# Batch norm with ReLU: all stores issued from GpSimd's queue in place of ScalarE's

## Chip, cores and metric

One core of a Trainium2 chip. The time is the device time of one execution in microseconds (us), the median of several, at a granted clock of 1.00. A profile is one execution under the hardware profiler; its span is the time from the first to the last instruction.

## The reference

```python
def setup_inputs():
    batch, channels, h, w = 32, 128, 32, 32
    # x (32,128,32,32) normal; gamma 1, beta 0, mean 0, var 1 (each of 128 channels); eps 1e-5

def reference(x, gamma, beta, running_mean, running_var, eps):
    normalized = (x - running_mean[None, :, None, None]) / np.sqrt(running_var[None, :, None, None] + eps)
    scaled = normalized * gamma[None, :, None, None] + beta[None, :, None, None]
    return np.maximum(scaled, 0).astype(np.float32)
```

16.78 MB of float32 are read, one multiply-add and a maximum made of each element, and 16.78 MB written.

## The kernel before

An image and channel is one row of 1024 elements; a partition holds 16 rows, and t numbers the two halves of the tensor. The first half is loaded in tiles that grow from 1 to 4 MB, the second as one 8 MB tile in two loads. All loads are issued from SyncE, the last by 8.5 us. ScalarE computes each tile in place and then issues its store; only the first tile has two stores. One store or load is cut into descriptors, pieces of 4 to 64 KB, which 16 transfer engines work through.

```python
J = 16
TILES = ((0, 0, 2), (0, 2, 4), (0, 4, 8), (0, 8, 16), (1, 0, 16))
LOAD_CUTS = {(1, 8)}
STORE_CUTS = {(0, 1)}
HALVES = {(0, 0), (0, 1)}
# ...
    for t, a, b in TILES:
        xt = data.tile([P, b - a, HW], F32, name=f"x{t}_{a}")
        cuts = [a] + [j for j in range(a + 1, b) if (t, j) in LOAD_CUTS] + [b]
        for c, d in zip(cuts, cuts[1:]):
            nc.sync.dma_start(out=xt[:, c - a : d - a, :], in_=xr[t, :, c:d, :])
        tiles.append((t, a, b, xt))
# ... scale_t and bias_t, one column per row, from the four parameters: done by 9.6 us
    with tc.manual_schedule(engines={mybir.EngineType.Activation}):
        for t, a, b, xt in tiles:
            first = a
            for j in range(a, b):
                step = HW // 2 if (t, j) in HALVES else HW
                for w in range(0, HW, step):
                    nc.scalar.activation(
                        out=xt[:, j - a, w : w + step], in_=xt[:, j - a, w : w + step],
                        func=ACTF.Relu, bias=bias_t[:, j : j + 1], scale=scale_t[:, j : j + 1],
                    )
                if j + 1 == b or (t, j + 1) in STORE_CUTS:
                    nc.scalar.dma_start(
                        out=outr[t, :, first : j + 1, :], in_=xt[:, first - a : j + 1 - a, :]
                    )
                    first = j + 1
```

Of the kernel before, what the change touches and what calls it, by code (L numbers as in the profile page):

```python
# [1 line left out]

# [4 lines left out]


F32 = mybir.dt.float32
ACTF = mybir.ActivationFunctionType  # L10
# [13 lines that stand above are left out]
@with_exitstack  # L24
def kernel(
    ctx: ExitStack,
    tc: tile.TileContext,
    x: bass.AP,
    gamma: bass.AP,
    beta: bass.AP,  # L30
    running_mean: bass.AP,
    running_var: bass.AP,
    eps: bass.AP,
    out: bass.AP,
):
    nc = tc.nc
    B, C, H, W = x.shape
    HW = H * W
    P = nc.NUM_PARTITIONS
    assert C % J == 0 and P % (C // J) == 0 and (B * C) % (P * J) == 0  # L40
    Q = C // J
    T = B * C // (P * J)

    xr = x.rearrange("b c h w -> (b c) (h w)").rearrange("(t p j) w -> t p j w", p=P, j=J)
    outr = out.rearrange("b c h w -> (b c) (h w)").rearrange("(t p j) w -> t p j w", p=P, j=J)

    data = ctx.enter_context(tc.tile_pool(name="data", bufs=1))
    params = ctx.enter_context(tc.tile_pool(name="params", bufs=1))
    psum = ctx.enter_context(tc.tile_pool(name="psum", bufs=1, space=bass.MemoryType.PSUM))

    tiles = []
# [9 lines that stand above are left out]
    raw = params.tile([Q, 4, J], F32, name="raw")  # L61
    for k, src in enumerate((running_var, gamma, running_mean, beta)):
        nc.scalar.dma_start(out=raw[:, k, :], in_=src.rearrange("(q j) -> q j", j=J))
    eps_t = params.tile([P, 1], F32, name="eps_t")
    nc.vector.memset(eps_t, float(eps))  # L65
    rep = params.tile([Q, P // Q, Q], F32, name="rep")
    nc.gpsimd.memset(rep, 1.0)  # L67
    nc.gpsimd.affine_select(  # L68
        out=rep,
        in_=rep,  # L70
        compare_op=mybir.AluOpType.is_equal,
        fill=0.0,
        base=0,
        pattern=[[0, P // Q], [-1, Q]],
        channel_multiplier=1,
    )
    cols = psum.tile([P, 4, J], F32, name="cols")
    nc.tensor.matmul(  # L78
        cols.rearrange("p k j -> p (k j)"),
        rep.rearrange("q r s -> q (r s)"),  # L80
        raw.rearrange("q k j -> q (k j)"),
        start=True,
        stop=True,
    )
    std_t = params.tile([P, J], F32, name="std_t")
    nc.scalar.activation(out=std_t, in_=cols[:, 0, :], func=ACTF.Sqrt, bias=eps_t[:, 0:1], scale=1.0)  # L86
    rstd_t = params.tile([P, J], F32, name="rstd_t")
    nc.vector.reciprocal(out=rstd_t, in_=std_t)  # L88
    scale_t = params.tile([P, J], F32, name="scale_t")
    nc.vector.tensor_mul(out=scale_t, in0=cols[:, 1, :], in1=rstd_t)  # L90
    ms_t = params.tile([P, J], F32, name="ms_t")
    nc.vector.tensor_mul(out=ms_t, in0=cols[:, 2, :], in1=scale_t)  # L92
    bias_t = params.tile([P, J], F32, name="bias_t")
    nc.vector.tensor_sub(out=bias_t, in0=cols[:, 3, :], in1=ms_t)  # L94

    with tc.manual_schedule(engines={mybir.EngineType.Activation}):
        for t, a, b, xt in tiles:
            first = a
            for j in range(a, b):
# [3 lines that stand above are left out]
                        out=xt[:, j - a, w : w + step],  # L103
                        in_=xt[:, j - a, w : w + step],
                        func=ACTF.Relu,
                        bias=bias_t[:, j : j + 1],
                        scale=scale_t[:, j : j + 1],
                    )
                if j + 1 == b or (t, j + 1) in STORE_CUTS:
                    nc.scalar.dma_start(  # L110
                        out=outr[t, :, first : j + 1, :], in_=xt[:, first - a : j + 1 - a, :]
                    )
                    first = j + 1


# [1 line left out]
_INS = ['x', 'gamma', 'beta', 'running_mean', 'running_var', 'eps']  # L117
_OUTS = [((32, 128, 32, 32), 'float32')]

_NUMBERS = {'eps': 1e-05}  # L120


# [26 lines left out]
```

## Time and profile before

| | before |
|---|---|
| time, three runs ahead of the prediction | 83.94 us (83.65 to 83.94) |
| span of the profile | 82.0 us |
| first load data, last store data (transfer records) | 1.80 us, 80.80 us |
| ScalarE busy | 39.1 us |
| loads and stores, share of the 16 transfer engines | 48.7% and 47.6% |
| last load ends, last store is issued | 46.2 us, 56.05 us |

How to read it: transfers are named by queue (q1 is SyncE's, q10 ScalarE's), and a queue's share is the time that its descriptors took on the 16 engines. The most useful view was the one that takes the queues in a chosen stretch of time: it shows what waits behind what. Its counts go by the start of a descriptor, so a short stretch can show over 100%. Two words are used below: the **stream** is the time from the first load data to the last store data, 79.00 us here, and the **close** is what follows to the end of the span, 1.17 us here. Both are taken from the trace's transfer records. A store's **landing** is the moment at which its semaphore is up: for the last store 0.34 us after its last data, so inside the close.

### The profile page before, as it was taken

What the parts mean: (1) busy time and instruction counts of PE and PEld (TensorE: products, weight loads), DVE (VectorE), ACT (ScalarE), POOL (GpSimd) and SP (SyncE); (2) the same over time, 40 slices, a digit from 0 to 9 for tenths busy, and PEclk for the clock granted to TensorE, in tenths of its full rate; (3) what the DMA queues carried; (4) which work ended last, traced back from release to release, by engine and by line L of the source; (5) the groups of instructions that cost most, each with busy time, mean ns of one, the idle gap of its engine ahead of it and who ended that gap; (6) DMA issues with size and microseconds to landing.
All of it is one profiled execution on the core that took longest, in us unless ns stands there. A gap on an engine that the chain in (4) does not pass through costs nothing.

```text
span 82.0 us, 120 instructions
## 1 busy us (share of the span) xinstructions
PE 0.7 (1%) x2; PEld 0.5 (1%) x2; DVE 0.8 (1%) x5; ACT 39.1 (48%) x36; POOL 0.8 (1%) x6
## 2 busy tenths in 40 slices
PE   0002000000000000000000000000000000000000
PEld 0002000000000000000000000000000000000000
DVE  0000300000000000000000000000000000000000
ACT  0600477799239999199994199993000000000000
POOL 3000000000000000000000000000000000000000
DMA  2899997979899989999799799998992999996590
GB/s 48 336 424 456 416 544 336 524 322 526 338 434 430 506 358 506 390 434 444 320 460 500 316 424 448 512 432 368 480 736 128 416 512 512 512 512 288 224 512 0
DMA packets 1792, 33.56 MB, mean 409 GB/s; under 512 B 256, under 2 KB 256, under 8 KB 512
## 3 DMA queue, kind: packets, MB, share of 16 engines
q1 hardware_dynamic: 864, 16.78, 48.7%
q10 hardware_dynamic: 928, 16.78, 47.6%
HBM read 16.78 MB, written 16.78 MB: 409 GB/s over the span
## 4 chain that ended last, share of the span: by engine, by line
DMA 56%; ACT 10%; issue 2%; SPq 0%
DMA x<-in_x_dram 56%; ACT x L102 10%; SPq L56 0%
## 5 line engine op out<-in xcount | busy, mean ns | idle before, releaser
L102 ACT ACTIVATE x<-x,bias_t,scale_t 128x1024 f32<-128x1024 f32 (+1 forms) x34 | 37.5, 1177 | 9.9 <-DMA x<-in_x_dram 7.6
L86 ACT ACT_TABLE_LOAD x1 | 1.3, 1283 | 2.6 <-issue 2.6
L86 ACT ACTIVATE std_t<-cols,eps_t 128x16 f32<-128x16 f32 x1 | 0.3, 273 | 4.5 <-PE cols L78 4.5
L78 PE MATMUL cols<-raw,rep 8*128 8x64 f32 x2 | 0.7, 429 | 7.6 <-DMA raw<-in_beta_dram 7.6
L78 PEld LDWEIGHTS cols<-raw,rep 8*128 8x128 f32 x2 | 0.5, 306 | 7.6 <-issue 7.6
L68 POOL TENSOR_SCALAR_AFFINE_SELECT rep<-rep 8x128 f32<-8x128 f32 x1 | 0.4, 392 | 0.1
L88 DVE RECIPROCAL rstd_t<-std_t 128x16 f32<-128x16 f32 x1 | 0.3, 254 | 7.7 <-ACT std_t L86 7.7
L67 POOL MEMSET rep<- 8x128 f32 x1 | 0.2, 194 | 0.3 <-POOLq L130 0.3
L90 DVE TENSOR_TENSOR scale_t<-cols,rstd_t 128x16 f32<-128x16 f32 x1 | 0.2, 175 | 0.1
L92 DVE TENSOR_TENSOR ms_t<-cols,scale_t 128x16 f32<-128x16 f32 x1 | 0.2, 175 | 0.0
L94 DVE TENSOR_TENSOR bias_t<-cols,ms_t 128x16 f32<-128x16 f32 x1 | 0.2, 174 | 0.0
L130 POOL MEMSET const-bfloat16-1.0<- 128x1 bf16 x1 | 0.1, 106 | 0.0
L130 POOL MEMSET const-uint8-127<- 128x1 uint8 x1 | 0.1, 106 | 0.0
L130 POOL MEMSET const-float32-0.0<- 128x1 f32 x1 | 0.1, 103 | 0.3 <-issue 0.3
L130 POOL MEMSET const-float32-1.0<- 128x1 f32 x1 | 0.1, 103 | 0.0
L65 DVE MEMSET eps_t<- 128x1 f32 x1 | 0.1, 59 | 0.9 <-PEq L130 0.9
## 6 DMA issues: line engine op xcount, KB each, us to landing
x<-in_x_dram SPq DMA_DIRECT2D x3, 4096.0 KB, 38.7
out_dram<-x ACTq DMA_DIRECT2D x1, 4096.0 KB, 28.7
x<-in_x_dram SPq DMA_DIRECT2D x2, 1024.0 KB, 5.8
x<-in_x_dram SPq DMA_DIRECT2D x1, 2048.0 KB, 11.3
out_dram<-x ACTq DMA_DIRECT2D x1, 2048.0 KB
out_dram<-x ACTq DMA_DIRECT2D x2, 512.0 KB, 19.6
out_dram<-x ACTq DMA_DIRECT2D x1, 1024.0 KB
raw<-in_running_var_dram ACTq DMA_DIRECT2D x1, 0.5 KB
```

Of the source, the lines that this page charges most:

```text
L65: nc.vector.memset(eps_t, float(eps))
L67: nc.gpsimd.memset(rep, 1.0)
L68: nc.gpsimd.affine_select(out=rep, in_=rep, compare_op=mybir.AluOpType.is_equal, fill=0.0, base=0, pattern=[[0, P // Q], [-1, Q]], channel ...
L78: nc.tensor.matmul(cols.rearrange("p k j -> p (k j)"), rep.rearrange("q r s -> q (r s)"), raw.rearrange("q k j -> q (k j)"), start=True, s ...
L86: nc.scalar.activation(out=std_t, in_=cols[:, 0, :], func=ACTF.Sqrt, bias=eps_t[:, 0:1], scale=1.0)
L88: nc.vector.reciprocal(out=rstd_t, in_=std_t)
L90: nc.vector.tensor_mul(out=scale_t, in0=cols[:, 1, :], in1=rstd_t)
L92: nc.vector.tensor_mul(out=ms_t, in0=cols[:, 2, :], in1=scale_t)
L94: nc.vector.tensor_sub(out=bias_t, in0=cols[:, 3, :], in1=ms_t)
L102: nc.scalar.activation(out=xt[:, j - a, w : w + step], in_=xt[:, j - a, w : w + step], func=ACTF.Relu, bias=bias_t[:, j : j + 1], scale=sc ...
L130: nc = _bacc.Bacc("TRN2", target_bir_lowering=False, num_devices=1)
```

## The change

The intent is to take the six store issues off ScalarE, which computes, and give them to GpSimd, which is idle. Nothing else is edited.

```diff
-    with tc.manual_schedule(engines={mybir.EngineType.Activation}):
+    with tc.manual_schedule(engines={mybir.EngineType.Activation, mybir.EngineType.Pool}):
         for t, a, b, xt in tiles:
# ...
                 if j + 1 == b or (t, j + 1) in STORE_CUTS:
-                    nc.scalar.dma_start(
+                    nc.gpsimd.dma_start(
                         out=outr[t, :, first : j + 1, :], in_=xt[:, first - a : j + 1 - a, :]
                     )
```

## The prediction

> **What bounds the kernel now.** I read the page first (busy shares, transfer queues, chain), then the queues in chosen stretches of time, then ScalarE's timeline. Busy shares, and the busy rows over the 40 slices:
>
> ```profile
> PE 0.7 (1%) x2; PEld 0.5 (1%) x2; DVE 0.8 (1%) x5; ACT 39.1 (48%) x36; POOL 0.8 (1%) x6
> ACT  0600477799239999199994199993000000000000
> DMA  2899997979899989999799799998992999996590
> ```
>
> The reader is to see that no engine is near full, ScalarE has nothing to do in the last 12 slices (25 us), and the transfer row is high from the second slice to the last but one. The dips in that row are partly an effect of counting: a long transfer is put where it starts, and one descriptor of the last store moves 64 KB and takes 2.4 us by the trace's transfer records. The queues over the whole span say how full the transfer engines are:
>
> ```profile
> q1 hardware_dynamic: 864, 16.78, 48.7%
> q10 hardware_dynamic: 928, 16.78, 47.6%
> HBM read 16.78 MB, written 16.78 MB: 409 GB/s over the span
> ```
>
> q1 holds the loads (issued by SyncE), q10 the stores and the four little parameter loads (issued by ScalarE). Together they fill 96.3% of the 16 transfer engines' 82.0 us, so 79.0 us; what is left, 3.0 us, is some 1.8 us before the first load moves (by the transfer records) and 1.2 us after the last store ended, at 80.8. So the bound is the transfer engines' own work: every byte read once and written once. The chain of waits agrees, with one trap:
>
> ```profile
> DMA x<-in_x_dram 56%; ACT x L102 10%; SPq L56 0%
> ```
>
> The chain ends in the last load and the eight ScalarE operations after it (to 56.03 us), and leaves the final 26 us, a store, without a name. Taken alone it says "a store issued earlier ends earlier". Whether that is so depends on the backlog of stores when the last one is issued, and so I looked at the queues in two stretches. First, before the loads end, 1.7 to 46.9 us:
>
> ```profile
> q1 hardware_dynamic: 864, 16.78, 88.4%
> q10 hardware_dynamic: 509, 2.33, 12.4%
> ```
>
> Then from there to the issue of the last store, 46.9 to 56.4 us:
>
> ```profile
> q10 hardware_dynamic: 203, 4.23, 103.4%
> ```
>
> By 46.9 us only 2.33 MB are written, though stores for 8.39 MB (0.5, 0.5, 1, 2 and 4 MB) have been issued, the 4 MB one last, at 33.10 us by ScalarE's timeline. So 6.06 MB are waiting, and from 46.9 on they alone keep the engines at 103% (counted by starts). At some 430 GB/s (33.56 MB in 77.9 us of descriptor time, which I summed from the records) they last 14.1 us, to 61.0 us. ScalarE's end of it:
>
> ```profile
> 34.85 9.16 ACT L102 ACTIVATE x<-x,bias_t,scale_t 128x1024 f32<-128x1024 f32 x8 [1.78 <-DMA x<-in_x_dram]
> 46.87 9.16 ACT L102 ACTIVATE x<-x,bias_t,scale_t 128x1024 f32<-128x1024 f32 x8 [2.86 <-DMA x<-in_x_dram]
> 56.05 0.34 ACTq L110 DMA_DIRECT2D out_dram<-x  x1
> ```
>
> The last store, 8.39 MB, is issued at 56.05 and done issuing at 56.39: 4.6 us before the backlog runs dry at 61.0. Its own data take 8 descriptors per engine of 2.418 us, 19.3 us: 61.0 + 19.3 = 80.3, where the records show 80.8. This slack of 4.6 us is the number on which everything below rests.
>
> **What the Trainium skill says.** Four places, all in its page "DMA: Bandwidth & Descriptors". (1) "Specifications" puts the latency to the first byte at about 1 us for a transfer issued from GpSimd, whose descriptors software writes, against about 0.6 us from SyncE or ScalarE. No transfer of data in this trace is issued from GpSimd, so nothing here shows it. (2) "Queues, rings and completion order" says that each transfer engine goes round the queues that have work, packet by packet, and that a packet may hold many descriptors. The trace shows the going round, with packets of one descriptor: from 14.6 to 35.5 us
>
> ```profile
> DMA packets 545, 8.90 MB, mean 426 GB/s; under 512 B 51, under 2 KB 51, under 8 KB 305
> q1 hardware_dynamic: 272, 7.86, 88.3%
> q10 hardware_dynamic: 273, 1.04, 12.1%
> ```
>
> has 305 - 51 = 254 store descriptors of 4 KB (the two 0.5 MB stores) against 7.86 MB / 32 KB = 240 load descriptors. It is one for one, and since a store's piece is an eighth of a load's, the loads get 7.86 of 8.90 MB. That is why there is a backlog. (3) "SWDGE vs HWDGE vs iDMA" has GpSimd's descriptors written to rings in SBUF, served in turn with the hardware queues by the same engines, in packets preferably of no more than 4096 B. My smallest store descriptor is 4096 B, so I expect one descriptor per packet again. (4) "Bandwidth", measured from GpSimd's queue: 16 MB at 425 GB/s. This kernel has 33.56 MB in 79.0 us, 425 GB/s, from the hardware queues: no lower rate is to be expected.
>
> **The change part by part.** It takes six store issues off ScalarE and puts them on GpSimd, each behind a semaphore from ScalarE. Sizes, order and buffers stay.
>
> Removed from ScalarE: 6 issues of 338 to 374 ns, 2.1 us, and the idle gaps behind the early ones, 1.3 us in 3 (operations waiting for their own earlier ones at the issue). Four issues stand between 9.6 and 21.3 us; without them ScalarE reaches the tile that starts at 23.91 some 2.5 to 3 us earlier and waits as much longer, for it waits for its load already (2.94 us). The last tile starts when its load lands, 46.87. Gain on the path: 0.
>
> Added on GpSimd: 6 issues. I take about 1 us each in place of 0.34, an estimate from place (1), not measured here. GpSimd has nothing after 1.5 us and idles between. A store becomes ready perhaps 1 to 1.5 us later than now after its last ScalarE operation. Early stores: each start that slips by a microsecond loses less than one 4 KB turn per engine (one per 1.213 + 0.159 = 1.37 us), the loads get the time, the engines stay full: 0. Last store: ready at 57 to 58 us in place of 56.4, before 61.0: 0, with 3 us to spare.
>
> Moved: the transfers go to another ring. Descriptor time 77.9 us per engine, unchanged if a descriptor costs what it does now: 0.
>
> At the end: the program must see the last store done. With GpSimd's queue the close may have one more step (its ring to be retired); from no row, I put +0.2 us. Sum: 83.94 + 0 + 0 + 0.2 = about 84.2 us.
>
> **Rivals.** *The order of service changes.* If a packet from GpSimd's ring held a whole store's share (8 descriptors), a store would be served at once in place of an eighth of its turn. Then up to 8.39 MB of stores would go before the loads end: 38.9 us of load descriptors plus 19.6 us of store descriptors (16 x 0.159 + 8 x (0.309 + 0.611 + 1.213)), loads ending near 60, ScalarE 9.2 us later, the last store at about 71, its 19.3 us and the close: 92 in place of 82, so some 94 us. For it: the many-descriptor packets of place (2). Against it: place (3), and 4 KB descriptors. I give 5%; half a change of this sort (2 or 3 descriptors a packet) would eat the slack and cost little.
>
> *A descriptor costs more.* There are 48 store descriptors per engine; with 50 ns more for each (fetching it from SBUF, say), 2.4 us, +2.9%. Against it: at 1.2 and 2.4 us a piece there is ample time to fetch ahead, and place (4). About 8%, and more for a smaller cost under 2%.
>
> *The start of the last store shows.* If GpSimd took over 4.6 us to start it, the engines would idle for the rest; six microseconds would cost 1.4. About 2%.
>
> *Faster.* The freed ScalarE could only help if it ended the last tile earlier, but that is bound to the load of 46.87 us and to 9.16 us of operations; and even then the backlog lasts to 61. 2%.
>
> **Range and chances.** Three runs of before lie within 0.3 us. Middle 84.2; low 83.5 (nothing at the end, a good run); high 86.0, which holds a small cost per descriptor or at the end, about 2 us. The limit of 2% is 85.6. Chances: faster 0.02, within 2% 0.82, slower 0.16.
>
> **What would show it.** In the profile after: a queue of another kind with 16.78 MB of stores and again near 48% for it and for the loads, with descriptors of the same sizes; one for one between 4 KB stores and 32 KB loads; the last load landing at 46 to 48 us; ScalarE's issues gone, with waits for loads longer by about as much; the last store issued by 58 us and its data until about 81. Wrong if the loads end later than 50 us (order of service), if the two queues' shares add up to over 80.5 us in place of 79.0 (cost per descriptor), if the transfer row shows a hole between 56 and 62 us (late start), or if more than 2 us lie between the last data and the end of the span (the close).

## The result, and the profile after

The changed kernel takes 84.41 us (84.35 to 84.46, 4 runs), the kernel before 83.80 us in the same rounds (83.62 to 83.94, 4 runs). The ratio is 1.0080, with a 95% interval of 1.0056 to 1.0104: slower by a little under one per cent, and "the same" at a limit of 2%. (A ratio is the mean time of one kernel's runs over that of the other's of the same rounds, so not quite the ratio of the medians.) The span grew from 82.0 to 82.6 us.

The page of the changed kernel, its queues over the whole span:

```profile
q1 hardware_dynamic: 864, 16.78, 48.5%
q0 software_dynamic: 864, 16.78, 47.2%
q10 hardware_dynamic: 64, 0.00, 0.0%
HBM read 16.78 MB, written 16.78 MB: 406 GB/s over the span
```

The stores are now in q0, of another kind (software), and take 47.2% of the longer span, as before. 864 packets are 48 data descriptors and 6 semaphore writes for each of 16 engines; the 64 left in q10 are the parameter loads. The records show the same five sizes of store descriptor with the same durations, to the nanosecond: 0.159, 0.309, 0.611, 1.213 and 2.418 us.

The queues in the changed kernel from 14.6 to 35.5 us:

```profile
DMA packets 525, 8.72 MB, mean 417 GB/s; under 512 B 48, under 2 KB 48, under 8 KB 289
q1 hardware_dynamic: 268, 7.73, 87.7%
q0 software_dynamic: 257, 0.99, 11.5%
```

289 - 48 = 241 store descriptors of 4 KB stand against 7.73 MB / 32 KB = 236 of the loads: one for one, as before. Up to 46.9 us, and then from 46.9 to 56.4 us, again in the changed kernel:

```profile
q0 software_dynamic: 434, 2.23, 11.8%
```

```profile
q0 software_dynamic: 207, 4.10, 100.2%
```

So the backlog is there too: 8.39 - 2.23 = 6.16 MB of stores wait when the loads end, and they keep the engines full past the issue of the last store. That issue, in the changed kernel's timeline, columns start and duration, beside ScalarE's last eight operations:

```profile
46.89 9.16 ACT L102 ACTIVATE x<-x,bias_t,scale_t 128x1024 f32<-128x1024 f32 x8 [2.92 <-DMA x<-in_x_dram]
56.34 0.53 POOL L110 DMA_DIRECT2D out_dram<-x  x1 [22.46 <-ACT x L102]
```

ScalarE's operations end at 56.05, GpSimd starts the issue 0.29 us later and takes 0.53 us (ScalarE took 0.34). The first data of this store move at 61.22 us (60.98 before), behind the backlog. Nothing so far costs time. The span's 0.68 us are made of two pieces: the stream is 0.18 us longer (79.18), and the close 0.49 us (1.66 in place of 1.17). For the close, the wait view of SyncE, which ends the program by waiting for everything; before, and then changed (total us, number of waits, longest):

```profile
SPq L144 <- DMA out_dram<-x: 72.5, 4, 38.9
```

```profile
SPq L144 <- DMA out_dram<-x: 75.7, 1, 75.7
```

Before, SyncE is held by stores four times; changed, once. The instructions of the closing line that end in the short stretch from the landing of the last store until SyncE has its list done say why; before (81.05 to 81.25 us), and changed (81.3 to 81.86 us). The columns are the engine's queue, the operation and its count, then shortest, median and longest in ns, and the first and last start:

```profile
L144 SPq EVENT_SEMAPHORE  x1: 28/28/28, 81.2 to 81.2; - x1
```

```profile
L144 SPq EVENT_SEMAPHORE  x8: 28/28/46551, 34.8 to 81.8; - x8
L144 POOLq DRAIN  x1: 25308/25308/25308, 56.3 to 56.3; - x1
```

Before, the wait for the last store stands last in SyncE's list, and those ahead of it are gone through while it is still in flight. In the changed kernel the first of eight waits is the one for the last store: it holds SyncE from 34.8 us for 46.55 us, and the seven others, all satisfied long ago, are stepped through after it, about 0.06 us each: 0.42 us. By the semaphores that the trace names, stores on the hardware queue reuse those of earlier transfers, while each of the six GpSimd stores has one of its own. GpSimd's own drain, the second line, also waits for its stores and ends at 81.63, 0.29 us after the last landing, but before SyncE's list is through at 81.85.

The steps after both took 0.74 us before and 0.80 in the changed kernel (among them a clearing of semaphores, 139 ns for 96, and a short drain, 102 ns for 77). With the 0.42 us this makes up the 0.49 but for 0.02.

That is a reading of one profile, and two theories can be told apart. **Queue of waits**: the close grows by the waits that stand behind the one for the last store. **GpSimd's ring**: it grows because a software queue must be retired.

### The profile page after: what moved, and what is told of

Its sections match the earlier page's. It is cut to its first block, busy times and chain, and to the rows that moved or that the text cites. A ratio compares the mean times of both kernels' runs of the same rounds, so it can differ in the third digit from the quotient of the medians.

```text
span 82.6 us, 125 instructions
## 1 busy us (share of the span) xinstructions
PE 0.7 (1%) x2; PEld 0.5 (1%) x2; DVE 0.8 (1%) x5; ACT 38.7 (47%) x36; POOL 4.2 (5%) x12
## 3 DMA queue, kind: packets, MB, share of 16 engines
q1 hardware_dynamic: 864, 16.78, 48.5%
q0 software_dynamic: 864, 16.78, 47.2%
## 4 chain that ended last, share of the span: by engine, by line
DMA 56%; issue 11%; POOLq 1%
DMA x<-in_x_dram 56%; POOLq L144 1%; POOLq L110 0%
## 5 line engine op out<-in xcount | busy, mean ns | idle before, releaser
L110 POOL DMA_DIRECT2D out_dram<-x x6 | 3.4, 559 | 52.0 <-ACT x L102 52.0
```

What stands on the lines that cost most here:

```text
L110: nc.gpsimd.dma_start(out=outr[t, :, first : j + 1, :], in_=xt[:, first - a : j + 1 - a, :])
```

## The experiments

Twelve runs were made, all correct; each ran beside the kernel before, on the same chip.

**e1: only the last store from GpSimd.**

```diff
-                    nc.gpsimd.dma_start(
+                    (nc.gpsimd if t == 1 else nc.scalar).dma_start(
```

> Only the last, 8 MB store is issued from GpSimd, the five others from ScalarE as before. Theory 'queue of waits' (the 0.5 us more at the close are SyncE's waits for other semaphores, which stand behind its wait for the last store: 7 of them in the changed kernel, none before, some 0.06 us each): here 2 stand behind it, so from the last data to the end of the span about 1.16 + 0.12 = 1.28 us, time +0.1 to +0.2 us against before. Theory 'GpSimd's ring' (retiring a transfer of GpSimd's queue costs it): the close is 1.65 us as in the changed kernel, time +0.5 or more. Theory 'late start' (a slow first transfer from GpSimd shows): over +1 us.

84.19 us, ratio 1.0052 (1.0029 to 1.0075). The close is 1.31 us. Of the closing line, from 81.25 to 81.45 us:

```profile
L144 SPq EVENT_SEMAPHORE  x3: 28/28/28922, 52.4 to 81.4; - x3
L144 POOLq DRAIN  x1: 24993/24993/24993, 56.3 to 56.3; - x1
```

One wait and two behind it, as expected. The drain ended 0.08 us after the last landing, not 0.29 as with six stores. So it is not a fixed cost of having used GpSimd's queue at the end. The close is 0.14 us longer than before, the time 0.48 us (84.19 beside 83.71). The rest is not in the span: over the runs of these rounds the mean span is 82.13 us beside 82.00, so 0.13 more, while the time less the span is 2.01 to 2.08 us here and 1.67 to 1.75 in the kernel before. It is 1.66 to 1.77 us in most kernels of this document, more in four: e1, e4 (1.81 to 1.87), e5 (1.85 to 2.05) and e8 (1.85 to 1.90). No run shows what makes it so; a difference in time of a few tenths is therefore not all to be looked for in the profile.

**e2: the reverse, the last store from ScalarE and the five others from GpSimd.**

```diff
-                    nc.gpsimd.dma_start(
+                    (nc.scalar if t == 1 else nc.gpsimd).dma_start(
```

> The reverse: the last store from ScalarE, the five others from GpSimd. 'Queue of waits': 5 waits stand behind the one for the last store, close about 1.16 + 0.30 = 1.46 us, time +0.3 to +0.5 us. 'GpSimd's ring': GpSimd's transfers are all done by 62 us, so the close is 1.16 us as before and the time +0 to +0.2 us (the 0.18 us of the stream, if that is of the queue).

84.25 us, ratio 1.0063 (1.0041 to 1.0085), close 1.53 us. From 81.47 to 81.87 us:

```profile
L144 SPq EVENT_SEMAPHORE  x6: 28/28/28, 81.5 to 81.8; - x6
```

And from 67.2 to 67.3 us:

```profile
L144 POOLq DRAIN  x1: 34158/34158/34158, 33.1 to 33.1; - x1
```

The wait for the last store has five behind it. GpSimd's drain was over at 67.25 us, 0.25 us after the landing of its own last store, and cannot have cost anything at 81. The ring theory, which wanted 1.16 us, fails as the cause of this close; the other wanted 1.46, 0.07 too little, as it left out the longer steps after the list.

In e1 and e2 the last store also has a queue to itself, beside the backlog in the other. Its first data still move only at 60.95 and 60.20 us, 4.6 and 4.0 us after the start of its issue. So a queue does not get its turns at once; the runs do not show what it waits for.

**e3: nine stores from GpSimd.** The early stores are cut into more pieces only so that the wait for the last store falls later in the list.

```diff
-STORE_CUTS = {(0, 1)}
+STORE_CUTS = {(0, 1), (0, 3), (0, 6), (0, 12)}
```

> All stores from GpSimd, the early ones cut into nine in all, so that the wait for the last store comes late in SyncE's list: 2 waits stand behind it in place of 7. 'Queue of waits': close about 1.28 us. 'GpSimd's ring': 1.65 us or more. The shorter descriptors add some 0.2 us of descriptor time per engine (16 x 0.159 - 8 x 0.309 = 0.07, 16 x 0.309 - 8 x 0.611 = 0.06, 16 x 0.611 - 8 x 1.213 = 0.07) under either theory.

84.34 us, ratio 1.0073 (1.0051 to 1.0096), close 1.53 us: neither 1.28 nor 1.65. From 81.5 to 81.95 us:

```profile
L144 SPq EVENT_SEMAPHORE  x3: 28/28/18928, 62.6 to 81.6; - x3
L144 POOLq DRAIN  x1: 26457/26457/26457, 55.5 to 55.5; - x1
```

Two waits stand behind, and SyncE's list is done at 81.70. But this time the drain is later: 55.47 + 26.46 = 81.93, 0.41 us after the last landing. So my theory was incomplete: both causes exist, they run side by side, and the later one sets the close.

**e4: the same nine stores from ScalarE.** The same cuts, applied to the kernel before.

> The same nine stores, all from ScalarE: GpSimd issues no transfer. Here 4 waits stand behind the one for the last store. 'Queue of waits': close about 1.16 + 0.24 = 1.40 us, longer than that of the nine stores from GpSimd. 'GpSimd's ring': 1.16 us. Descriptor time +0.2 us as in the run before it.

84.73 us, ratio 1.0120 (1.0094 to 1.0145), close 1.42 us (1.40 expected). From 81.9 to 82.26 us:

```profile
L144 SPq EVENT_SEMAPHORE  x5: 28/28/33939, 48.0 to 82.2; - x5
```

Here no transfer is issued from GpSimd, and the close is still 0.25 us longer than before, with four waits behind it. The list alone does it, and the steps after it take 0.75 us, as before.

**e5 to e8: is there slack, and what does a start from GpSimd cost?** Three or eight further operations, Relu of what is already Relu, delay the last store on ScalarE; e5 and e7 are built on the kernel before, e6 and e8 on the changed one.

```diff
+                if t == 1 and j + 1 == b:
+                    for _ in range(3):    # 8 in e7 and e8
+                        nc.scalar.activation(
+                            out=xt[:, j - a, :], in_=xt[:, j - a, :], func=ACTF.Relu
+                        )
                 if j + 1 == b or (t, j + 1) in STORE_CUTS:
```

> Stores from ScalarE; three more ScalarE operations of 1.22 us (Relu of what is already Relu) are put ahead of the last store, which is then issued 3.7 us later, at some 59.7 us. Theory 'backlog' (the last store's issue has slack until the earlier stores run dry at 61.0): no change, 83.8 us +-0.2. Rival 'the issue sets the end': +3.7 us, 87.5.

> The same three operations in the changed kernel; the last store is issued at 60.0 us from GpSimd. 'Backlog': first data about 1.3 us after the start of the issue, 61.3, where the backlog ends at about 61.1: within +0.5 us of the changed kernel (84.4 to 84.9). 'The issue sets the end': +3.7, 88.1.

> Eight such operations: the last store is issued at some 65.9 us, with the backlog gone since 61.0. 'Backlog': the transfer engines stand idle until about 66.8 (0.94 us from issue to first data, as the first load has it), so +5.8 us, about 89.6. 'The issue sets the end': +9.8, 93.6. It also measures the start of a store from ScalarE on idle transfer engines.

> The same eight in the changed kernel: the last store is issued at some 66.1 us on idle engines. It measures the disputed start of a store from GpSimd: about 0.3 us of hop from ScalarE and 1.3 us from the start of the issue to the first data (my estimate), so +6.4 us against the changed kernel, about 90.8, and 0.6 us more idle than the run before. If GpSimd's start took over 4 us, as the rival of the late start needs, it would be 94 or more.

An added operation takes 1.08 us, not the 1.22 of the others, so the delays are 3.3 and 8.9 us. e5: 83.95 us, 0.38% over the kernel before (0.16 to 0.60%). Its issue in the timeline, and the stretches up to the backlog's end and just after (from and to, length, busy us of five engines, granted clock, the transfer engines' share, GB/s; counted by starts, so over 1 is possible):

```profile
59.34 0.34 ACTq L115 DMA_DIRECT2D out_dram<-x  x1
46.90:60.90 14.00, 0.00 (x0) 0.00 (x0) 0.00 (x0) 12.31 (x11) 0.00 (x0) 1.00 1.01 435
60.90:62.00 1.10, 0.00 (x0) 0.00 (x0) 0.00 (x0) 0.00 (x0) 0.00 (x0) 1.00 2.21 953
```

The last store is issued at 59.34 and its first data move at 60.97, where it was 60.98 without the delay: the 3.3 us are hidden. (By the ratio the time is 0.32 us longer, outside my +-0.2; of this some 0.2 us lie outside the span, as in e1: the mean span is 81.95 us beside 81.87.) e6: 84.47 us, ratio 1.0099 (1.0072 to 1.0126), beside 84.41 of the changed kernel without the delay, in other rounds; first data at 61.35. With eight operations the backlog runs out, at 61.8 us. From two views of e7 (stores from ScalarE), the issue in the timeline and the stretches behind the backlog's end (columns as for e5):

```profile
64.91 0.34 ACTq L115 DMA_DIRECT2D out_dram<-x  x1
62.00:65.70 3.70, 0.00 (x0) 0.00 (x0) 0.00 (x0) 2.82 (x3) 0.00 (x0) 1.00 0.00 0
65.70:66.30 0.60, 0.00 (x0) 0.00 (x0) 0.00 (x0) 0.00 (x0) 0.00 (x0) 1.00 4.09 1748
```

The same of e8 (stores from GpSimd):

```profile
65.21 0.53 POOL L115 DMA_DIRECT2D out_dram<-x  x1 [31.57 <-ACT x L111]
62.00:65.70 3.70, 0.00 (x0) 0.00 (x0) 0.00 (x0) 2.85 (x3) 0.49 (x1) 1.00 0.00 0
65.70:66.30 0.60, 0.00 (x0) 0.00 (x0) 0.00 (x0) 0.00 (x0) 0.04 (x1) 1.00 0.00 0
```

The engines stand idle until 65.75 us in e7 and 66.31 in e8. From the start of the issue to the first data it is 0.84 us from ScalarE and 1.10 from GpSimd; from the end of ScalarE's last operation, 0.87 and 1.39, because of the hop of 0.29. So a store on the path starts 0.52 us later from GpSimd, by one profile of each. The times are 88.20 (1.0558) and 89.31 us (1.0683): below my 89.6 and 90.8, as the delay was 0.9 us shorter and the backlog lasted 0.8 us longer than I had put in. Of the 1.1 us between them, 0.56 are the later first data, 0.25 the close and 0.2 lie outside the span. "The issue sets the end" wanted the full delay in e5 and e6; it fails.

**e9 and e10: both kernels again, unchanged**, for the stream.

> The kernel before, unchanged, as a yardstick of the same chip: ratio 1.000 +-0.002, close 1.16 us, and a second reading of the stretch from the first to the last data (79.00 us in the first profile, 79.18 in that of the changed kernel).

> The changed kernel, unchanged: ratio 1.008 +-0.002, close 1.66 us. If the 0.18 us of the stream belong to GpSimd's queue, the stretch is again some 0.2 us longer than that of the run before this one; if they are scatter from run to run, the two overlap.

e9: 83.59 us, ratio 0.9993 (0.9976 to 1.0010), stream 78.82, close 1.18. e10: 84.38 us, ratio 1.0086 (1.0072 to 1.0100), stream 79.31, close 1.66. The close repeats to 0.01 us, the result to 0.0006. The stream is again longer with GpSimd's stores, by 0.49 us this time.

**e11: all stores from SyncE**, in the same queue as the loads.

```diff
-                    nc.scalar.dma_start(
+                    nc.sync.dma_start(
```

(and SyncE in place of GpSimd in the list of engines in program order)

> All stores from SyncE, behind the loads in the same queue: the strongest change of the order of service. Theory 'the transfer engines are the bound, and any order serves that keeps them full': the loads end by 42 us in place of 46 (38.9 us of descriptors from 1.8, no stores between), the last store is issued at about 51, and the time is 83.8 us within 0.5%, with the close of before (the wait for the last store stands last). Rival 'the order of service sets the end' (stores must go beside loads): slower by over 2%.

84.56 us, ratio 1.0115 (1.0096 to 1.0135): between the two expectations, a miss by over half a per cent. The queues from 1.7 to 42 us, with no stores among the loads:

```profile
DMA packets 912, 16.78 MB, mean 416 GB/s; under 512 B 144, under 2 KB 144, under 8 KB 144
q1 hardware_dynamic: 848, 16.78, 101.2%
```

The loads do go first, and the first 4 KB store starts at 42.33 us; the last load ends at 42.98, a microsecond later than expected. No hole follows and the close is that of the kernel before (1.17), so a wholly different order of service keeps the engines full. But the stream is 79.99 us: by the records, load descriptors took 1.79 us per engine more than their usual 0.309, 0.611 and 1.213 us, in place of 0.95 in the first profile, and 0.9 of it falls after 40 us, in the last of the loads.

**e12: seventeen stores from GpSimd**, for the drain.

```diff
-STORE_CUTS = {(0, 1)}
+STORE_CUTS = {(0, j) for j in range(16)}
```

> Seventeen stores from GpSimd, for the other part of the close: GpSimd's drain came 0.08, 0.29 and 0.41 us after the last landing with 1, 6 and 9 stores. If it costs some 0.042 us for each transfer that it issued, it comes 0.75 us after here, the close is about 0.34 + 0.75 + 0.76 = 1.85 us (1.53 with nine). If it costs a fixed time, or only the last eight count, 1.5 us. All stores but the last have 4 KB descriptors: 128 x 0.159 - 19.6 = +0.74 us per engine. Time about +1.4 to +1.7 us against before.

85.15 us, ratio 1.0182 (1.0161 to 1.0203), close 1.84 us. From 81.85 to 82.65 us:

```profile
L144 SPq EVENT_SEMAPHORE  x3: 28/28/18895, 63.0 to 82.0; - x3
L144 POOLq DRAIN  x1: 27129/27129/27129, 55.5 to 55.5; - x1
```

SyncE has its list done at 82.05; the drain ends at 55.48 + 27.13 = 82.61, 0.74 us after the last landing, where 0.75 was expected. GpSimd's drain costs some 0.04 us for each transfer that it issued, those long complete included: in these five kernels (1, 5, 6, 9 and 17 transfers) it ends 0.08, 0.25, 0.29, 0.41 and 0.74 us after the landing of GpSimd's own last store.

The closes that tell the theories apart (us):

| kernel | waits behind | stores from GpSimd | SyncE's list done, after last landing | drain ends, after last landing | close |
|---|---|---|---|---|---|
| before; e9 | 0 | 0 | 0.09; 0.09 | none | 1.17; 1.18 |
| e1 | 2 | 1 | 0.19 | 0.08 | 1.31 |
| e4 | 4 | 0 | 0.33 | none | 1.42 |
| e2 | 5 | 5 | 0.39 | 14 us before it | 1.53 |
| changed; e10 | 7 | 6 | 0.51; 0.51 | 0.29; 0.29 | 1.66; 1.66 |
| e3 | 2 | 9 | 0.18 | 0.41 | 1.53 |
| e12 | 2 | 17 | 0.18 | 0.74 | 1.84 |

The others: 1.16 (e5) and 1.17 us (e11) with no wait behind, 1.64 (e6) and 1.65 (e8) with seven, as the kernels that they are built on. Only e7 differs, 1.40 where 1.17 is due: SyncE's list is done 0.09 us after the last landing, so the 0.23 us more come after the list, and I have no cause for them.

**The stream stays open.** With the early stores from ScalarE it was 79.00, 78.82, 79.12 (e1) and 79.19 us (e5), mean 79.03; with them from GpSimd 79.18, 79.31, 79.33 (e2) and 79.43 (e6), mean 79.31. The 0.28 us lie mostly in load descriptors that take longer than usual. After 40 us, these overruns are 0.10, 0.00, 0.09 and 0.13 us per engine in the first four, and 0.16, 0.48, 0.36 and 0.40 in the others; e7 and e8, whose streams hold idle time, have 0.10 and 0.41. But with nine stores it is the other way round: the stream is 79.78 us from ScalarE (e4, overruns 0.53) and 79.36 from GpSimd (e3, 0.41), of which 0.2 us each are the shorter descriptors. And e12, all from GpSimd, has 79.72 us, of which 0.74 are its shorter descriptors; e11, with no store from GpSimd, has overruns of 0.90. So it is not GpSimd's queue as such. It may go with how loads and stores meet near the end of the loads, but these runs do not show that.

No experiment beat the kernel before, and none pointed to a version that would: 77.9 us of its 83.6 are descriptors at their usual durations.

## Why the prediction was right

Predicted were 84.2 us, 83.5 to 86.0, with 82% for "within 2%"; measured 84.41 us and a ratio of 1.008. That the middle came within 0.2 us is partly luck: the working added 0.2 us where 0.6 came (84.41 beside 83.80), and the base of 83.94 was 0.14 too high. That nothing on the path costs more than some tenths is the part that was worked out, and it held.

- **The bound.** The step "the bound is the transfer engines' own work" held: the same bytes in the same descriptors with the same durations. Shares of 48.5% and 47.2% of 82.65 us are 79.1 us, where it said 79.0. (Its 77.9 us "of descriptor time" are the sum at usual durations; the records of the first profile sum to 78.85, with the loads' overruns of 0.95.)
- **The slack of 4.6 us.** Shown by delay: 3.3 us on the last store moved its first data by 0.01 us in e5, and 8.9 us emptied the engines in e7, where it moved by 4.8. So 4.1 us were hidden, not 4.6: the number left out that data follow the end of an issue only 0.5 us later (0.84 us from its start). The chain of waits, which names the last load and ScalarE, would have sent a reader to speed up an issue that is worth nothing.
- **Order of service.** One descriptor for one, as expected; last load 46.20 us (46.17 before). Equal counts show equal turns; that a packet held one descriptor, and not the same few in both queues, is not shown. The rival of 94 us is refuted.
- **Removed from ScalarE.** 0 on the path, right. Its step "some 2.5 to 3 us earlier" was too large: ScalarE waits 4.44 us for the load at 23.9 in place of 2.94, so 1.5. I had added the issues and the idle gaps behind them, but an issue is not counted as busy, so the gap of 0.45 us contains it. Off the path this did no harm.
- **Added on GpSimd.** The term "about 1 us each" measured 0.53 us (the first 0.69), with 0.29 of hop; the last store's issue was over at 56.9, before the 57 to 58 predicted. On an idle engine it would have cost 0.52 us (e8 against e7); here the backlog hid it.
- **Descriptor cost.** Store descriptors cost no more, by their median to the nanosecond; the rival is refuted. (Place (4) of the prediction is a figure for loads; that it carries over to stores is shown only here.) Of the "0" put down for the stream, 0.18 to 0.49 us are left over, and unexplained.
- **At the end.** The term "+0.2 us" for a ring to be retired was mis-sized and its cause half wrong: the close grew by 0.49 us. Seven waits behind the one for the last store make 0.42 of it, and longer steps after them 0.06; the retiring is real, 0.29 us for six stores, but hidden behind the waits.

## What to carry to other kernels

Where the transfer engines are full from end to end and a backlog of stores stands in front of the last one, as here, the queue that issues a store mattered little (0.8%): first compute the backlog at the last issue, and only then ask what an issue costs. A chain of waits that ends long before the span does need not name the bound. And a difference of half a microsecond that is always there may lie in the last two microseconds of the trace: where the wait for the last store stands in the closing list, and how many transfers the software queue has to retire. Compare the time less the span too: part of a difference can lie outside the profile (0.3 us in e1).

## What the Trainium skill lacked or had wrong

- No page that I found has the price of each GpSimd transfer at a program's close: GpSimd's drain ended 0.08, 0.29, 0.41 and 0.74 us after the last landing with 1, 6, 9 and 17 transfers, though most were complete long before. It would belong in "DMA: Bandwidth & Descriptors".
- Nor did I find one that tells that the closing waits are stepped through one after the other, at about 0.06 us each, and that a list headed by the last transfer's semaphore costs all the others (seven: 0.42 us).
- "DMA: Bandwidth & Descriptors", "Specifications": about 1 us to the first byte from GpSimd and 0.6 from the hardware queues, without saying from when it counts. From the start of the issue I have 1.10 and 0.84 us (e8 and e7) on idle engines; the difference is 0.26 us rather than 0.4, and the hop from ScalarE, 0.29 us, counts as much.
- The same page, "Queues, rings and completion order", gives many descriptors per packet as typical. With descriptors of 4 KB and more, both kinds of queue went one for one with the loads (254 to 240, and 241 to 236). A line on how the share of the engines then goes by descriptor size would help: 4 KB stores got 1.04 of 8.90 MB beside 32 KB loads.
